# Summing rows of 1024 numbers: the input stream staged through two buffers of 24 rows in place of three of 16

## The chip, the cores and the metric

One NeuronCore of a Trainium2 chip runs the kernel. The metric is the device time of one execution in microseconds (us), taken as the median of several runs. The other cores are idle in these runs.

## The reference

```
x: float32 [32, 512, 1024], divisor = 1024
out[b, s] = sum(x[b, s, :]) / divisor        # float32 [32, 512]
```

So 16,384 rows of 1024 floats (4 KB each, 67.1 MB in all) are read, and one number per row is written.

## The kernel before, in words

The 16,384 rows are spread over the 128 partitions of the on-chip memory, 128 rows to a partition (`J = 128`). A partition's rows come from two places in the input: `F = 15` rows from a first region (`x_first`, where partition p starts p x 15 rows in), and `W = M + L = 113` rows from a second region (`x_main`, `M = 97` rows, followed for each partition by `x_last`, `L = 16` rows). In what follows "a row" means one row in each partition, that is 128 x 4 KB = 512 KB.

The input passes through three buffers, `bulk0` to `bulk2`, of 16 rows each (64 KB per partition). The list `loads` (lines 101 to 112) gives the order: 2 rows, five times 16 rows and 15 rows of the main region, then the 15 rows of the first region, then the last 16 rows cut in four: 10.6 rows (called `t8` in the code) and 3.7 rows (`t9`) into bulk buffers, and two small pieces, `pa` (5376 bytes per partition) and `pb` (1664 bytes), into buffers of their own. Each load names its buffer, one semaphore per buffer, its source, how many of its rows ScalarE sums (`on_act`: 4 of the last main load, 6 of the first region's load) and where the sums go.

There is no scheduler: each engine's queue is written out by hand, and semaphores order them.

- **SyncE (SP)** issues every DMA. The first two loads are moved ahead of the program's opening barrier (`start_loads_at_once`). Load 2 waits until load 0 has landed (line 138); from load 3 on, load k waits (lines 140 to 143) until the engines have finished with load k - 3, which held the same buffer. `pa` and `pb` follow load 9 with no wait of their own. Then SP waits for GpSimd and stores the first region's results, waits for `pa` and stores the main results, and waits for `done` and stores the last 16 columns.
- **VectorE (DVE)** takes the loads in order: one `reduce_sum` (line 215) per load over all its rows, less those that go to ScalarE. The last 16 rows are summed one at a time by `both_halves` (line 205), which adds the two halves of a row and accumulates.
- **ScalarE (ACT)** sums single rows by an activation with an accumulator (line 183): the `on_act` rows of two loads, and six of the last 16 rows.
- **GpSimd (POOL)** multiplies the finished sums by 1/1024 (lines 157 and 161).

Of the kernel before, what the change touches and what calls it, by code (L numbers as in the profile page):

```python
# [35 lines left out]
def kernel(  # L36
# [6 lines left out]
    nc = tc.nc  # L43
    nc.at_finalize(start_loads_at_once)
    xf = x.flatten_outer_dims()
    N, D = xf.shape
# [2 lines left out]
    J = N // P  # L49
    assert J * P == N  # L50

    F, L = 15, 16
    M = J - F - L
    W = M + L
    x_first = bass.AP(tensor=x.tensor, offset=0, ap=[[F * D, P], [1, F * D]])
# [1 line left out]
    x_last = bass.AP(tensor=x.tensor, offset=P * F * D + M * D, ap=[[W * D, P], [1, L * D]])  # L57
# [4 lines left out]
    def room(name, *shape):  # L62
        return nc.alloc_sbuf_tensor(name, [P, *shape], F32).ap()
# [2 lines left out]
    base = -(-nc.sbuf_base // 32) * 32  # L66
    room("pad", -base % 1024 // 4)
    assert nc.sbuf_base % 1024 == 0
    bulk = [room(f"bulk{i}", 16 * D) for i in range(3)]

# [2 lines left out]
    ends = [0, 10 * D + c10, 14 * D + c14, 15 * D + c15, 16 * D]  # L75
# [11 lines left out]
    loads = []  # L87
    sems = {}

    def sem(name):  # L90
        sems[name] = nc.alloc_semaphore(name)
        return sems[name]

    in_bulk = [sem(f"in_bulk{i}") for i in range(3)]
    in_pa, in_pb = (sem(f"in_{n}") for n in ("pa", "pb"))
    out_first, out_main = sem("out_first"), sem("out_main")
    dve, act, pool = sem("by_dve"), sem("by_act"), sem("by_pool")
    done = sem("done")
    landed = nc.alloc_semaphore("landed")

    main = [(2, 0)] + [(16, 0)] * 5 + [(15, 4)]
    first = [(15, 6)]
    assert sum(r for r, _ in first) == F and sum(r for r, _ in main) == M
    for rows_of, src, dst in ((main, x_main, res), (first, x_first, res0)):
        j = 0
        for rows, on_act in rows_of:
            t = bulk[len(loads) % 3][:, : rows * D]
            loads.append((t, in_bulk[len(loads) % 3], src[:, j * D : (j + rows) * D], on_act, dst[:, j : j + rows]))
            j += rows
    for k in range(2):  # L110
        t = bulk[len(loads) % 3][:, : ends[k + 1] - ends[k]]
        loads.append((t, in_bulk[len(loads) % 3], x_last[:, ends[k] : ends[k + 1]], 0, None))


    for t, s, src, *_ in loads[:2]:
        i = nc.sync.dma_start(out=t, in_=src).then_inc(s, 16)
        tc.no_tile_sem_insts.add(i.ins.name)
    tc.close()
    tc.compile()  # L119
# [2 lines left out]
    done_dve, done_act = {}, {}  # L122
# [4 lines left out]
    arrived, seen = [], {}  # L127
# [6 lines left out]
    for k, (t, s, src, *_) in enumerate(loads):  # L134
        if k < 2:
            continue
        if k == 2:
            nc.sync.wait_ge(loads[0][1], arrived[0])
        else:
            nc.sync.wait_ge(dve, done_dve[k - 3])  # L140
            if done_act[k - 3]:
                nc.sync.wait_ge(act, done_act[k - 3])
            nc.sync.wait_ge(s, arrived[k] - 16)
        nc.sync.dma_start(out=t, in_=src).then_inc(s, 16)
    nc.sync.dma_start(out=pa, in_=x_last[:, ends[2] : ends[3]]).then_inc(in_pa, 16)
    nc.sync.dma_start(out=pb[:, : D - c15], in_=x_last[:, ends[3] : ends[4]]).then_inc(in_pb, 16)
    nc.sync.wait_ge(pool, 3)
# [6 lines left out]
    k = len(main) - 1  # L154
# [31 lines left out]
    for k, (t, s, src, on_act, dst) in enumerate(loads[:-2]):  # L186
        rows = t.shape[1] // D
# [23 lines left out]
    for k, (t, s, src, on_act, dst) in enumerate(loads[:-2]):  # L211
        m = t.shape[1] // D - on_act
        nc.vector.wait_ge(s, arrived[k])
        rows = t[:, : m * D].rearrange("p (r d) -> p r d", d=D)
# [65 lines left out]
```

## Time and profile before

| what | value |
|---|---|
| median of three runs | 160.39 us (160.37 to 160.51) |
| span of the profiled execution, first to last instruction | 159.3 us |
| VectorE busy | 116.7 us (73%) |
| ScalarE busy | 18.6 us (12%) |
| DMA engines: packets, data, share of the span | 2160, 67.18 MB, 98.1% |
| mean rate over the span | 422 GB/s |

The profile is of one execution, and its page gives that execution's span but no time of its own for what lies outside the span. The median run is 1.1 us longer than the span (160.39 - 159.3); in what follows that 1.1 us is carried along unchanged.

The DMA engines' packets are also recorded one by one in the trace, with start, length and size. In these loads a packet is one descriptor: one partition's contiguous piece of a load, so a 16-row load is 128 packets of 65,536 bytes, eight for each of the 16 DMA engines. Eight is also the number of partitions that each engine serves.

### The profile page before, as it was taken

Reading aid. Unit: us, or ns where it says so; the run is one execution under the profiler, and the core shown is the slowest. Engines: PE = TensorE matmul, PEld = TensorE weight load, DVE = VectorE, ACT = ScalarE, POOL = GpSimd, SP = SyncE. Lnnn points to the kernel's source line nnn. Section 1 sums busy time; section 2 is a strip of 40 time slices with the busy share of each in tenths; the row PEclk is TensorE's granted clock in tenths of the full one; section 3 lists DMA queues with packets and bytes.
Section 4 is the critical chain, followed back from the end, with each engine's and each line's share of the span. In section 5 each row is a group of like instructions: output and inputs, shape, how many; then the busy total and the mean of one; then the engine's idle time right before and its main releaser. Section 6 shows DMA issues by size and latency. Waiting matters only on the chain.

```text
span 159.3 us, 144 instructions
## 1 busy us (share of the span) xinstructions
DVE 116.7 (73%) x32; ACT 18.6 (12%) x35; POOL 1.0 (1%) x7
## 2 busy tenths in 40 slices
DVE  0500009999499994999949999499989990399296
ACT  3000000000000000000000000000009100392196
POOL 0000000000000000000000000000000001000000
DMA  8996996996996997979969969969996999889894
GB/s 296 494 527 263 527 527 263 527 527 263 527 527 263 527 444 346 527 313 477 527 263 527 527 263 527 494 278 463 494 494 262 478 494 494 350 350 525 344 401 154
DMA packets 2160, 67.18 MB, mean 422 GB/s; under 512 B 624, under 2 KB 752, under 8 KB 880
## 3 DMA queue, kind: packets, MB, share of 16 engines
q1 hardware_dynamic: 2160, 67.18, 98.1%
HBM read 67.11 MB, written 0.07 MB: 422 GB/s over the span
## 4 chain that ended last, share of the span: by engine, by line
DMA 67%; DVE 30%; another core or an unknown queue 1%; issue 0%
DMA bulk<-in_x_dram 67%; DVE res L215 29%; DVE bulk L205 1%; DVE tail L205 0%; DVE pb L205 0%; DVE fin L205 0%
## 5 line engine op out<-in xcount | busy, mean ns | idle before, releaser
L215 DVE TENSOR_REDUCE res<-bulk 128x16 f32<-128x16384 f32 (+3 forms) x8 | 110.0, 13754 | 37.7 <-DMA bulk<-in_x_dram 37.7
L183 ACT ACTIVATE junk<-bulk 128x1024 f32<-128x1024 f32 (+1 forms) x16 | 15.6, 973 | 137.2 <-DMA bulk<-in_x_dram 137.2
L205 DVE CUSTOM_DVE_ANT_0 bulk<-bulk 128x512 f32<-128x512 f32 (+1 forms) x9 | 5.5, 665 | 3.1 <-DMA bulk<-in_x_dram 3.1
L183 ACT ACTIVATION_READ_ACCUMULATOR junk<-bulk 128x1 f32 x16 | 3.0, 187 | 0.0
L183 ACT ACT_TABLE_LOAD x1 | 1.3, 1283 | 1.9 <-PEq L119 1.9
L157 POOL TENSOR_SCALAR res<-res 128x97 f32<-128x97 f32 x1 | 0.5, 465 | 129.8 <-DVE res L215 129.8
L205 DVE DVE_READ_ACCUMULATOR2_ANT fin<- 128x1 f32 x10 | 0.8, 82 | 0.0
L183 ACT ACTIVATE junk<-tail 128x737 f32<-128x737 f32 x1 | 0.8, 789 | 0.0
L205 DVE CUSTOM_DVE_ANT_0 bulk<-bulk,part 128x192 f32<-128x192 f32 x1 | 0.4, 420 | 0.3 <-DMA bulk<-in_x_dram 0.3
L205 DVE CUSTOM_DVE_ANT_0 tail<-tail 128x304 f32<-128x304 f32 x1 | 0.5, 476 | 0.0
L205 DVE CUSTOM_DVE_ANT_0 pb<-pb 128x209 f32<-128x209 f32 x1 | 0.4, 379 | 0.1
L161 POOL TENSOR_SCALAR res<-res 128x15 f32<-128x15 f32 x1 | 0.3, 262 | 15.6 <-DVE res L215 15.6
L183 ACT ACTIVATION_READ_ACCUMULATOR junk<-tail 128x1 f32 x1 | 0.2, 187 | 0.0
L153 POOL MEMSET pb<- 128x2 f32 x1 | 0.1, 99 | 1.5 <-POOLq L119 1.5
L261 POOL MEMSET const-bfloat16-1.0<- 128x1 bf16 x1 | 0.1, 101 | 0.0
L261 POOL MEMSET const-uint8-127<- 128x1 uint8 x1 | 0.1, 101 | 0.0
L261 POOL MEMSET const-float32-0.0<- 128x1 f32 x1 | 0.1, 98 | 0.2 <-issue 0.2
L261 POOL MEMSET const-float32-1.0<- 128x1 f32 x1 | 0.1, 98 | 0.0
L205 DVE DVE_READ_ACCUMULATOR2_ANT pb<- 128x1 f32 x1 | 0.1, 84 | 0.0
L205 DVE DVE_READ_ACCUMULATOR2_ANT part<- 128x1 f32 x1 | 0.1, 83 | 0.0
## 6 DMA issues: line engine op xcount, KB each, us to landing
bulk<-in_x_dram SPq DMA_DIRECT2D x2, 7680.0 KB, 39.3
bulk<-in_x_dram SPq DMA_DIRECT2D x1, 5440.0 KB, 32.0
bulk<-in_x_dram SPq DMA_DIRECT2D x1, 1872.0 KB, 23.5
bulk<-in_x_dram SPq DMA_DIRECT2D x1, 1024.0 KB, 4.6
tail<-in_x_dram SPq DMA_DIRECT2D x1, 672.0 KB, 24.7
pb<-in_x_dram SPq DMA_DIRECT2D x1, 208.0 KB, 24.8
bulk<-in_x_dram SPq DMA_DIRECT2D x5, 40.8
out_dram<-res SPq DMA_DIRECT2D x1, 48.5 KB, 1.6
```

The source lines that it names most:

```text
L153: nc.gpsimd.memset(pb[:, D - c15 :], 0.0).then_inc(pool)
L157: nc.gpsimd.tensor_scalar_mul(out=res, in0=res, scalar1=scale).then_inc(pool)
L161: nc.gpsimd.tensor_scalar_mul(out=res0, in0=res0, scalar1=scale).then_inc(pool)
L183: nc.scalar.activation(scratch, src, COPY, scale=by, accum_out=dst).then_inc(count)
L205: return nc.vector.tensor_tensor_reduce(out=src[:, :h], in0=src[:, :h], in1=src[:, h:], scale=by, scalar=ahead, op0=ADD, op1=ADD, accum_ou ...
L215: nc.vector.reduce_sum(out=dst[:, :m], in_=rows, axis=AX).then_inc(dve)
L261: nc = _bacc.Bacc("TRN2", target_bir_lowering=False, num_devices=1)
```

## The change

The three buffers of 16 rows become two of 24 (192 KB per partition in all, as before). The loads become 2 rows, four times 24 rows of the main region, 14 rows of the first region, and the last 16 rows as they were: ten loads of input in place of twelve. A 24-row load is 96 KB per partition, and is written as an access pattern of two pieces of 48 KB. ScalarE sums 12 rows of the last 24-row load and 5 of the 14-row load. From load 2 on, load k waits for the engines to be done with load k - 2.

```diff
-    F, L = 15, 16
+    F, L = 14, 16
...
-    bulk = [room(f"bulk{i}", 16 * D) for i in range(3)]
+    bulk = [room(f"bulk{i}", 24 * D) for i in range(2)]
...
-    main = [(2, 0)] + [(16, 0)] * 5 + [(15, 4)]
-    first = [(15, 6)]
+    main = [(2, 0)] + [(24, 0)] * 3 + [(24, 12)]
+    first = [(14, 5)]
...
+    def load(t, src):
+        if t.shape[1] > 16 * D:
+            t, src = (v.rearrange("p (c f) -> p c f", c=2) for v in (t, src))
+        return nc.sync.dma_start(out=t, in_=src)
 
     for t, s, src, *_ in loads[:2]:
-        i = nc.sync.dma_start(out=t, in_=src).then_inc(s, 16)
+        i = load(t, src).then_inc(s, 16)
...
-        if k == 2:
-            nc.sync.wait_ge(loads[0][1], arrived[0])
-        else:
-            nc.sync.wait_ge(dve, done_dve[k - 3])
-            if done_act[k - 3]:
-                nc.sync.wait_ge(act, done_act[k - 3])
-            nc.sync.wait_ge(s, arrived[k] - 16)
-        nc.sync.dma_start(out=t, in_=src).then_inc(s, 16)
+        nc.sync.wait_ge(dve, done_dve[k - 2])
+        if done_act[k - 2]:
+            nc.sync.wait_ge(act, done_act[k - 2])
+        nc.sync.wait_ge(s, arrived[k] - 16)
+        load(t, src).then_inc(s, 16)
```

Elsewhere `% 3` becomes `% 2`. With F = 14, M becomes 98 and W becomes 114, so a partition's starting points in the input lie 114 rows (456 KB) apart in the second region in place of 113 (452 KB), and 14 rows (56 KB) in the first in place of 15 (60 KB). VectorE's instructions become one reduce of 2 rows, three of 24, one of 12 and one of 9, where they were 2, five of 16, 11 and 9; ScalarE sums 17 rows ahead of the last 16 where it summed 10. The work on the last 16 rows is the same, instruction for instruction.

More of the change, by code (lines that the diff above doesn't have):

```diff
@@ L92, in sem @@
         return sems[name]
-    in_bulk = [sem(f"in_bulk{i}") for i in range(3)]
+    in_bulk = [sem(f"in_bulk{i}") for i in range(2)]
     in_pa, in_pb = (sem(f"in_{n}") for n in ("pa", "pb"))
@@ L106 @@
         for rows, on_act in rows_of:
-            t = bulk[len(loads) % 3][:, : rows * D]
-            loads.append((t, in_bulk[len(loads) % 3], src[:, j * D : (j + rows) * D], on_act, dst[:, j : j + rows]))
+            t = bulk[len(loads) % 2][:, : rows * D]
+            loads.append((t, in_bulk[len(loads) % 2], src[:, j * D : (j + rows) * D], on_act, dst[:, j : j + rows]))
             j += rows
     for k in range(2):
-        t = bulk[len(loads) % 3][:, : ends[k + 1] - ends[k]]
-        loads.append((t, in_bulk[len(loads) % 3], x_last[:, ends[k] : ends[k + 1]], 0, None))
+        t = bulk[len(loads) % 2][:, : ends[k + 1] - ends[k]]
+        loads.append((t, in_bulk[len(loads) % 2], x_last[:, ends[k] : ends[k + 1]], 0, None))
+    def load(t, src):
+        if t.shape[1] > 16 * D:
+            t, src = (v.rearrange("p (c f) -> p c f", c=2) for v in (t, src))
+        return nc.sync.dma_start(out=t, in_=src)
     for t, s, src, *_ in loads[:2]:
-        i = nc.sync.dma_start(out=t, in_=src).then_inc(s, 16)
+        i = load(t, src).then_inc(s, 16)
         tc.no_tile_sem_insts.add(i.ins.name)
```

## The prediction

> **What bounds the kernel now.** I read the page's slices first, then its DMA table, then the packets in the trace. The slices show one resource that never rests:
>
> ```profile
> span 159.3 us, 144 instructions
> ...
> DVE  0500009999499994999949999499989990399296
> ...
> DMA  8996996996996997979969969969996999889894
> ...
> q1 hardware_dynamic: 2160, 67.18, 98.1%
> ```
>
> VectorE has holes (the 4s: it waits for each load). The DMA row's 6s are no holes: a 64 KB packet is booked in one slice and the slices are not multiples of it. Asked stage by stage (columns: stretch, its length, busy time of DVE, ACT and POOL, clock, DMA share, GB/s), the trace gives:
>
> ```profile
> 42.60:81.30 38.70, 34.44 (x2) 0.00 (x0) 0.00 (x0) 1.00 1.00 432
> ...
> 118.90:137.10 18.20, 11.89 (x1) 4.27 (x8) 0.47 (x1) 1.00 1.00 434
> ...
> 149.90:154.30 4.40, 3.48 (x11) 3.48 (x7) 0.00 (x0) 1.00 1.01 432
> ```
>
> The DMA share is 1.00 wherever loads follow loads, whether the load is 16 rows, 15 or 3.7. The timeline says what VectorE does meanwhile, and how the end hangs on the stream:
>
> ```profile
> 4.61 2.29 DVE L215 TENSOR_REDUCE res<-bulk 128x2 f32<-128x2048 f32 x1 [4.61 <-DMA bulk<-in_x_dram]
> ...
> 43.28 17.22 DVE L215 TENSOR_REDUCE res<-bulk 128x16 f32<-128x16384 f32 x1 [2.13 <-DMA bulk<-in_x_dram]
> 62.65 17.22 DVE L215 TENSOR_REDUCE res<-bulk 128x16 f32<-128x16384 f32 x1 [2.15 <-DMA bulk<-in_x_dram]
> ...
> 119.83 11.89 DVE L215 TENSOR_REDUCE res<-bulk 128x11 f32<-128x11264 f32 x1 [1.04 <-DMA bulk<-in_x_dram]
> ...
> 137.99 9.76 DVE L215 TENSOR_REDUCE res<-bulk 128x9 f32<-128x9216 f32 x1 [6.26 <-DMA bulk<-in_x_dram]
> ...
> 155.28 0.42 DVE L205 CUSTOM_DVE_ANT_0 bulk<-bulk,part 128x192 f32<-128x192 f32 x1 [0.29 <-DMA bulk<-in_x_dram]
> ...
> 157.85 0.33 SPq L238 DMA_DIRECT2D out_dram<-fin  x1
> ```
>
> Loads land 19.37 us apart (43.28 to 62.65) and are reduced in 17.22, so VectorE waits 2.1 us each time. From t9's landing at 155.28 a fixed string of work leads to the last store at 157.85 and the end of the span, 4.0 us after that landing. So the time is t9's landing + 4.0 + 1.1 outside the span, and the landing is set by the stream: when it starts, what each packet costs, and whether it pauses.
>
> **Packets.** In the trace's packet records the median lengths are 2.418 us for 65,536 bytes, 2.267 for 61,440, 1.608 for 43,520, 0.559 for 14,976, 0.309 for 8,192 and 0.069 for 1,664. A line through them: bytes / 27.2 GB/s + 0.008 us. Eight 64 KB packets are 19.344 us; the first packets of successive 16-row loads start at 23.24, 42.57, 61.96, 81.30, 100.67, that is 19.33 to 19.39 apart. Nothing is lost between loads: a load's border costs each engine some 0.007 us, its semaphore packet.
>
> **The change part by part.**
>
> *Removed and added packets.* Per partition the input was 12 packets (1 + 5 + 2 + 2 + 2) and becomes 14 (1 + 8 + 1 + 2 + 2). Two more, times eight partitions per engine, times 0.008 us: +0.13 us. Two load borders fewer: -0.01. The bytes are the same. The 48 KB packet is in no row; from its neighbours (43,520 and 61,440) the line gives 1.815 us, and 0.008 is what every size shows, so I take +0.12 us. Were its fixed part nil, the term would be -0.01; were it the 0.07 of a whole 1,664-byte packet, +1.0. I take the line because it holds over a forty-fold range of sizes.
>
> *Slow packets.* In the records some packets are longer than their median. Summed and shared over 16 engines that is 0.14 us in the 16-row loads (mean 2.4216 against 2.418, forty per engine), 0.18 in the two 15-row loads (2.278 against 2.267, sixteen), and about 0.03 in the rest of the stream. The new stream may have none (-0.35) or twice as many (+0.35). I see no reason for either and take 0.
>
> *The start.* Loads 0 and 1 still stand first. The trace's first packet starts at 1.00 us and load 1's at 3.92 us, while load 1 is issued by 0.85; a longer issue for its 256 packets has 3 us of cover. Load 2 now waits for load 0's reduce (6.9 us) instead of its landing (4.6); load 1 keeps the engines busy until 33, so 0.
>
> *The reduces.* 16 rows take 17.22 us and 2 rows 2.286: 1.067 a row and 0.15 fixed. So 24 rows take 25.75, 12 rows 12.95. VectorE saves some fixed parts, all in its own idle time: 0. ScalarE's 12 rows at 1.04 apart (12.5 us) stay under VectorE's 12.95, its 5 rows under 9.76: 0. GpSimd's two multiplies change by one column: 0.
>
> *The new waits.* This is the part that could cost. SP now issues load k + 1 only when load k - 1 is reduced, while load k is moving. Behind SP's wait stand all later loads; who suffers is the stream, if load k is out of packets before load k + 1's first one starts. Timed from load k - 1's last packet: 0.37 us until VectorE starts (the record of that packet's semaphore, 62.28, to 62.65), 25.75 for the reduce, 0.04 for SP to see it, and then issue to first packet. That last step the trace shows only on an idle queue: 1.00 us at the start, 0.83 at the last store (157.85 to 158.68). In sum 27.16. Load k has packets for 16 x 1.815 + 0.01 = 29.05 us, and the earliest engine is 0.32 ahead of the last (61.96 to 62.28): 28.73. **Slack 1.6 us.** Loads 3, 4 and 5 have this. Load 6 (t8) waits for 12 rows' reduce while the 14-row load moves (16.94 us): 2.3 us. Load 7 (t9) waits for 9 rows' reduce, 9.76, while t8 moves, 12.87: 12.87 - 0.32 - 0.37 - 9.76 - 0.04 - 1.00 = 1.4 us, the least. `pa` and `pb` are issued right behind t9, about 16 us later than before, and the first region's store after them; pb's issue ends about 1.3 us after t9's begins, and t9 only starts moving 2.4 us after its issue: 0. So I price the hand-offs at 0; if a busy queue takes over 2.4 us from issue to first packet, that is gone.
>
> *Strides.* A partition's pieces start 456 KB apart for 452, and 56 KB for 60. No row shows an even number of rows. The two strides shown, 113 and 15 rows, give 18.26 and 18.20 us of packets per engine for the two 15-row loads, 0.3% apart, and that is the bound either way: 0.3% of 154 us is 0.5 us. [...]
>
> [...]
>
> **Sum.** +0.12 + 0 + 0 + 0: 160.39 + 0.12 = 160.5 us; in the profile, t9 lands near 155.4 and the span is near 159.4. The median of a few runs tells about 0.2% (0.32 us) from nothing, so this is "the same".
>
> **Rivals.**
>
> 1. *The hand-off loses read-ahead* (slower). With one load queued instead of two, an engine crossing a load's border may have to ramp as it did at the start: there eight 8 KB packets took 2.935 us per engine and not 8 x 0.309 = 2.472, a loss of 0.46. At five late-issued loads that is 2.3 us: 162.8. For it: no row shows a load issued under 10 us ahead of its turn, besides the first two. Against it: 1.4 us are left, and the start's ramp also holds the first memory access of all. It decides from 2.4 us between issue and first packet. Chance 0.08.
> 2. *A loaded memory answers later* (slower). The 1.00 us from issue to first packet was on idle engines. Were it three times that while 16 engines stream, 3.0 us, three hand-offs would fall short by 0.4 (3.0 against 2.6) and t9's by 0.6: +1.8 us with the packets' 0.12 on top, 162.3. Twice, 2.0 us, would cost nothing. Against it: with 432 GB/s moving, borders cost nothing, though those loads were queued long before. Chance 0.06. [...]
> 3. *Strides or slow packets*, with their 0.3 to 0.5 us, shift the stream beyond what can be told: 161.0 with chance 0.08, 160.0 with chance 0.06.
> 4. *The descriptors are not two of 48 KB* but cut finer, say six of 16 KB: 4 loads x 8 partitions x 4 more x 0.008 = 1.0 us, 161.5. The built program shows the pattern 128x2x12288, which speaks for two. Chance 0.02.
>
> **How the numbers follow.** The forecast, no hand-off loss and packets on the line, has 0.70. Faster by over 0.2% is rival 3's lower end, 0.06; slower is 1, 2, 3's upper end and 4, with 0.24; within 0.2%, 0.70. The range takes the forecast's 160.1 to 160.8 and rival 3's ends, with small shortfalls of rivals 1 and 2 (a hand-off or two at 0.3 us): 160.0 to 161.2.
>
> **What would show it.** DMA packets 2384 in the table (2160 + 8 x 128 - 6 x 128 - 2 x 16); DMA share about 98%; 24-row reduces of about 25.75 us with VectorE idle 3.3 us before each; loads landing 29.05 us apart; 1.00 in every stretch between 4 and 154 us; t9's reduce at 155.4. I am wrong on the packets if loads are 29.05 apart plus more with the share still 1.00; on the hand-offs if the share falls under 1.00 around 33, 62, 91, 120, 137 or 150 us, where one load ends and the next begins.

## The result, and the profile after

The changed kernel takes 163.19 us (median of five runs, 162.87 to 163.55) against 160.39 us (160.36 to 160.75): slower by 1.7%, ratio 1.0172 with a 95% interval of 1.0157 to 1.0186. The forecast was 160.5 us with a range of 160.0 to 161.2.

The profiled run took 162.87 us, its span is 161.3 us. A second profile of the kernel before, taken with the last experiments, comes from a run of 160.40 us and has a span of 159.1 us. By the traces the spans are 161.34 and 159.07 us. So 2.3 of these 2.5 us lie in the span, and 0.2 outside of it (1.5 against 1.3 us), where the profile shows nothing. The comparison below uses this second profile where it needs a clean one: the first had some slow packets in its 15-row loads (2.278 us on average for a median of 2.267).

The page of the changed kernel:

```profile
span 161.3 us, 153 instructions
...
DVE  0500000069999974999999099999937994599185
...
DMA  8999999999999999999999999999999998989892
...
DMA packets 2384, 67.18 MB, mean 416 GB/s; under 512 B 592, under 2 KB 720, under 8 KB 848
...
q1 hardware_dynamic: 2384, 67.18, 97.5%
```

Read alone, this looks like what was forecast: 2384 packets, and a DMA row of nines to the end. A pause of a us on a few of 16 engines doesn't show in slices of 4 us. VectorE's instructions do show it, since each of its reduces starts when the last of the 16 engines has brought its part (load 3's last packet ends at 92.45 in the packet records, and its reduce starts at 92.80; the number in brackets is VectorE's idle time before):

```profile
33.72 25.75 DVE L217 TENSOR_REDUCE res<-bulk 128x24 f32<-128x24576 f32 x1 [26.71 <-DMA bulk<-in_x_dram]
62.70 25.75 DVE L217 TENSOR_REDUCE res<-bulk 128x24 f32<-128x24576 f32 x1 [3.24 <-DMA bulk<-in_x_dram]
92.80 25.75 DVE L217 TENSOR_REDUCE res<-bulk 128x24 f32<-128x24576 f32 x1 [4.35 <-DMA bulk<-in_x_dram]
121.83 12.95 DVE L217 TENSOR_REDUCE res<-bulk 128x12 f32<-128x12288 f32 x1 [3.27 <-DMA bulk<-in_x_dram]
139.13 9.75 DVE L217 TENSOR_REDUCE res<-bulk 128x9 f32<-128x9216 f32 x1 [4.35 <-DMA bulk<-in_x_dram]
152.47 0.49 DVE L207 CUSTOM_DVE_ANT_0 bulk<-bulk 128x320 f32<-128x320 f32 x1 [3.58 <-DMA bulk<-in_x_dram]
157.10 0.42 DVE L207 CUSTOM_DVE_ANT_0 bulk<-bulk,part 128x192 f32<-128x192 f32 x1 [0.46 <-DMA bulk<-in_x_dram]
```

Load 2, the last one issued early, lands 28.98 us after load 1, as 16 packets of 1.815 us per engine should. Load 3, the first one issued late, takes 30.10 (+1.1); load 4 29.03; the 14 rows 17.30 (+0.4 on 8 x 2.117); t8 13.34 and t9 4.63, where the second profile of before has 12.83 and 4.42 (+0.5 and +0.2). Together that is about the 2.1 us by which t9 lands later, at 157.10 against 155.01; from there to the end of the span it is 4.2 us against 4.1. What these five have in common is that they were issued late. The chain that ended last passes through three of them, loads 3, 5 and t9 (start, length, what):

```profile
33.72 25.76 DVE res L217
59.48 0.02 issue
59.49 33.28 DMA bulk<-in_x_dram
92.78 0.02 issue
92.80 25.77 DVE res L217
118.57 0.02 issue
118.59 20.52 DMA bulk<-in_x_dram
139.11 0.02 issue
139.13 9.77 DVE res L217
148.90 0.02 issue
148.91 8.16 DMA bulk<-in_x_dram
```

The chain goes from a reduce to the issue of the next load but one, and from the issue to that load's landing. Before, such a stretch began at an issue some 20 us ahead of the load's turn; in the first profile's chain, that of load 6 (15 rows) is

```profile
79.89 39.92 DMA bulk<-in_x_dram
```

of which its own packets are 18.3 us. In the changed kernel's three stretches, take off each load's own packets (29.05, 16.94, 4.47) and the 0.37 us until VectorE starts, and what is left of 33.28, 20.52 and 8.16 is 3.9, 3.2 and 3.3 us: the time from SP's issue until the slowest engine moves the load at its full rate. The prediction had 1.00 us there, from issue to first packet.

The packet records show the same place from the other side. In load 4, issued at 88.49 with the stream reaching it at 91.18, 15 of the first 48 packets are late: 14 of them are long, up to 2.23 us for a median of 1.815, and one starts 0.5 us after its engine's last one ended. (The records don't name the engine; packets were strung together by their ends and starts. "Late" is used below for packets over 0.04 us longer than their size's median, or starting over 0.03 us after the one before, among the first 48 of a load. "Lead" is the time from a load's issue to the first packet of it that any engine starts.) The leads of loads 3 to 7 were 2.5, 2.7, 1.7, 2.4 and 1.2 us. The engines are not alike in this: in load 5, by the same stringing, 13 of the 16 engines lost nothing, with only 1.7 to 2.9 us between the issue and their own turn, and the other three lost 0.2 to 0.8 us. The landing goes by the last engine to end, at 138.81 where the first ends at 137.22; VectorE's reduce starts at 139.13.

### The profile page after: what moved, and what is told of

Same layout as the page of the kernel before. It is cut to its first block, busy times and chain, and to the rows that moved or that the text cites. A ratio compares the mean times of both kernels' runs of the same rounds, so it can differ in the third digit from the quotient of the medians.

```text
span 161.3 us, 153 instructions
## 1 busy us (share of the span) xinstructions
DVE 108.9 (68%) x30; ACT 25.9 (16%) x49; POOL 1.0 (1%) x7
## 2 busy tenths in 40 slices
DMA packets 2384, 67.18 MB, mean 416 GB/s; under 512 B 592, under 2 KB 720, under 8 KB 848
## 3 DMA queue, kind: packets, MB, share of 16 engines
q1 hardware_dynamic: 2384, 67.18, 97.5%
## 4 chain that ended last, share of the span: by engine, by line
DMA 59%; DVE 38%; ACT 1%; issue 1%; SPq 0%
DMA bulk<-in_x_dram 59%; DVE res L217 38%; ACT junk L185 1%; SPq L118 0%
## 5 line engine op out<-in xcount | busy, mean ns | idle before, releaser
L217 DVE TENSOR_REDUCE res<-bulk 128x24 f32<-128x24576 f32 (+3 forms) x6 | 102.3, 17042 | 46.6 <-DMA bulk<-in_x_dram 46.6
L185 ACT ACTIVATE junk<-bulk 128x1024 f32<-128x1024 f32 (+1 forms) x23 | 22.6, 983 | 131.7 <-DMA bulk<-in_x_dram 131.7
L185 ACT ACTIVATION_READ_ACCUMULATOR junk<-bulk 128x1 f32 x23 | 4.3, 187 | 0.0
L159 POOL TENSOR_SCALAR res<-res 128x98 f32<-128x98 f32 x1 | 0.5, 465 | 132.8 <-DVE res L217 132.8
```

Of the source, the lines that this page charges most:

```text
L159: nc.gpsimd.tensor_scalar_mul(out=res, in0=res, scalar1=scale).then_inc(pool)
L185: nc.scalar.activation(scratch, src, COPY, scale=by, accum_out=dst).then_inc(count)
L217: nc.vector.reduce_sum(out=dst[:, :m], in_=rows, axis=AX).then_inc(dve)
```

## The experiments

Theory A is what this reading suggests: a load issued only some 3 us ahead of its turn reaches some engines late. Rivals: B, the strides of 114 and 14 rows make packets slow; C, only t9 and the small transfers behind it suffer. All ratios are to the kernel before, with 95% intervals.

**1. ScalarE helps, so that loads 3 to 5 are issued earlier.**

```diff
-    main = [(2, 0)] + [(24, 0)] * 3 + [(24, 12)]
+    main = [(2, 0)] + [(24, 8)] * 3 + [(24, 12)]
```

> ScalarE takes 8 rows of each of the first three 24-row loads, so VectorE's reduce there is 16 rows (about 17.2 us instead of 25.75) and SP issues loads 3, 4 and 5 about 11.8 us before the load ahead of them has landed, instead of 3.2. t9 is still issued late. Theory A (a load issued only some 3 us ahead of its turn reaches some of the 16 DMA engines late, and these stay behind to the end): the slow first packets at 62, 91 and 120 us go, the loads' landings stay 29.05 apart, and the time falls by 1.0 to 1.5 us from 163.2, to 161.7 to 162.2, the rest staying with t9. Theory B (the row strides of 114 and 14 make packets slow): unchanged, 163.2. Theory C (only the late issue of t9 and of the small transfers behind it costs): unchanged, 163.2.

Measured: 162.27 us, 1.0109 (1.0092 to 1.0127). That is just above the 161.7 to 162.2 that A gave. Leads of loads 3 to 5 are 10.9 us and none of their first 48 packets is late. What stays is at the end: t8 lands 13.77 us after the 14 rows (+0.9) and t9 4.71 after t8 (+0.3). B and C both said 163.2; C can still be right in part.

**2. t9 behind t8 in the same buffer, so that t9, pa and pb are issued early.**

```diff
+        s = in_bulk[len(loads) % 2]
+        if k == 1:
+            t, s = bulk[0][:, ends[1] : ends[2]], in_t9
...
+        if k < len(loads) - 1:
             nc.sync.wait_ge(dve, done_dve[k - 2])
```

> t9 goes into the free part of bulk0 behind t8, with a semaphore of its own, so t9, pa and pb are issued right behind t8 near 135 us instead of 149 us; loads 3, 4 and 5 are issued as late as in the changed kernel. Theory A: t9's slow packets (up to 0.92 us against 0.559) go, the time falls by 0.5 to 0.9 us, to 162.3 to 162.7. Theory B: unchanged, 163.2. Theory C: all of the loss goes, 160.5.

Measured: 162.79 us (161.52 to 163.18), 1.0129 (1.0101 to 1.0158), 0.1 us above the 162.3 to 162.7 that A gave, with the runs far apart. t8 and t9 now land 12.84 and 4.46 us apart, without loss, but in this profile the 14-row load, with a lead of 1.6 us, lost 1.6 (121.97 to 140.50 is 18.53). VectorE's rows and the DMA share around it (columns as in the prediction):

```profile
121.97 12.95 DVE L222 TENSOR_REDUCE res<-bulk 128x12 f32<-128x12288 f32 x1 [3.39 <-DMA bulk<-in_x_dram]
...
140.50 9.76 DVE L222 TENSOR_REDUCE res<-bulk 128x9 f32<-128x9216 f32 x1 [5.57 <-DMA bulk<-in_x_dram]
```

```profile
93.50:119.50 26.00, 25.08 (x1) 0.00 (x0) 0.00 (x0) 1.00 0.98 423
119.50:122.50 3.00, 0.53 (x1) 0.53 (x1) 0.00 (x0) 1.00 1.05 377
122.50:125.00 2.50, 2.50 (x1) 2.50 (x5) 0.00 (x0) 1.00 0.75 275
```

The share of 0.75 between 122.5 and 125 proves little by itself, since a whole packet is booked in one window and these windows are short. The kernel before reads 0.76 where its packet records show no wait over 0.2 us:

```profile
119.50:122.50 3.00, 2.67 (x1) 2.67 (x5) 0.00 (x0) 1.00 0.76 328
```

What shows the loss is the landing, 18.53 us after load 4's, and the packet records, by which all 16 engines lost on this load, 0.5 to 2.0 us each. C falls: with t9 mended most of the loss remains.

**3. Both edits.**

> Both edits: no load is issued less than about 5 us ahead of its turn. Theory A: 160.4 to 160.7, the packets' own 0.1 us being all that is left. Theory B: unchanged, 163.2. Theory C: 160.5, the same as with t9 alone moved.

Measured: 160.82 us, 1.0028 (1.0016 to 1.0040). B falls, since the strides are those of the change: about five sixths of the 2.8 us are gone with them in place. 0.1 us more than A's upper end is left. Part of what is left can't come from a short lead: load 4, issued 10.9 us ahead, landed 29.39 us after load 3 (29.28 in experiment 1), because a few packets in its later part were slow. Why they were, no run here shows.

**4. The strides of before, the late issues of the change.**

```diff
-    F, L = 14, 16
+    F, L = 15, 16
...
-    main = [(2, 0)] + [(24, 0)] * 3 + [(24, 12)]
-    first = [(14, 5)]
+    main = [(2, 0)] + [(24, 0)] * 3 + [(23, 12)]
+    first = [(15, 6)]
```

> The strides of the kernel before (113 rows in the second region, 15 in the first), with two buffers of 24 rows and late issues as in the changed kernel; the last main load is 23 rows and the first region's 15. Theory A: unchanged, 163.0 to 163.4. Theory B: 160.4 to 160.7. Theory C: unchanged.

Measured: 165.85 us, 1.0314 (1.0279 to 1.0350), which neither theory said. The old strides help nothing, against B. That it got slower has a reason that the edit brought along: load 4 has 23 rows and moves 1.2 us less, while load 5 still waits for 24 rows' reduce. Its lead fell to 1.0 us, with 32 late packets and gaps of up to 2.9 us on single engines, and it landed 20.43 us after load 4 (+2.3 on 18.14).

**5 and 6. How much lead is enough: one row or two rows on ScalarE.** As experiment 3, with `(24, 1)` and `(24, 2)` for `(24, 8)`.

> As the kernel with both edits (t9 behind t8, ScalarE helping with the first three 24-row loads), but ScalarE takes 1 row of each of these loads instead of 8. SP issues loads 3, 4 and 5 about 3.5 us before the stream reaches them (2.4 with no row, 10.9 with eight). Theory A, sharpened from the packet records (on the slowest engine a load issued into a busy queue needs 3.3 to 3.9 us until its first packet moves at full rate, not 1.0): most of the loss goes, a few late packets are left; 160.9 to 161.6. If the queue must instead hold several packets ahead (a need that grows with the lead, not a threshold): 161.8 to 162.2.

> The same with 2 rows on ScalarE: lead about 4.6 us, above the 3.9 us. Theory A with the threshold: as with eight rows, 160.7 to 160.9, and no late first packets at 62, 91 and 120 us. A need that grows with the lead: 161.3 to 161.7.

Measured: 160.67 us, 1.0016 (1.0007 to 1.0026) with one row, and 160.82 us, 1.0028 (1.0016 to 1.0041) with two. One row is as good as eight, and better than the 160.9 to 161.6 that A gave. With it the three leads are 3.41 to 3.47 us and no packet of the three loads is late:

```profile
62.79 24.69 DVE L222 TENSOR_REDUCE res<-bulk 128x23 f32<-128x23552 f32 x1 [4.32 <-DMA bulk<-in_x_dram]
91.84 24.69 DVE L222 TENSOR_REDUCE res<-bulk 128x23 f32<-128x23552 f32 x1 [4.36 <-DMA bulk<-in_x_dram]
120.83 12.95 DVE L222 TENSOR_REDUCE res<-bulk 128x12 f32<-128x12288 f32 x1 [4.30 <-DMA bulk<-in_x_dram]
```

The loads land 29.05 and 28.99 apart. 1.07 us of reduce per load (25.75 to 24.69) with t9 moved is worth 2.5 us. So the need for many packets in the queue, which would have left 161.8 to 162.2, falls: about 3.4 us of lead was enough, where 2.3 to 2.7 us lost 0.3 to 1.1 us on load 3 (the change and experiments 2, 4, 8 and 9). The border isn't sharp. t8's lead of 3.1 us in these two runs cost 0.3 and 0.4 us, while t8 in experiment 3 (lead 2.7) and the 14 rows in experiment 9 (lead 2.4) landed without loss.

**7. The reverse: the kernel before, issuing one load later.**

```diff
-            nc.sync.wait_ge(dve, done_dve[k - 3])
-            if done_act[k - 3]:
-                nc.sync.wait_ge(act, done_act[k - 3])
+            nc.sync.wait_ge(dve, done_dve[k - 2])
+            if done_act[k - 2]:
+                nc.sync.wait_ge(act, done_act[k - 2])
```

> The kernel before (three buffers of 16 rows, strides 113 and 15) with one change: load k waits for the engines to be done with load k - 2, as in the changed kernel, though a third buffer lies free. A 16-row load moves for 19.35 us and is reduced in 17.22, so the lead is about 1.4 us. Theory A: a load that starts 2 us late gives the next one 2 us more lead, so about every other of six hand-offs loses some 2 us on its slowest engines: 163.5 to 166.5, with gaps of 1 to 3 us in the packet records where loads meet. Theory B (strides, packet sizes or two buffers as such): unchanged, 160.4.

Measured: 166.87 us, 1.0389 (1.0348 to 1.0430), a little above the expected range. Three buffers, 64 KB packets and the old strides are all in place; the wait alone costs 6.5 us, over twice what the whole change does, with leads of 1.0 to 1.9 us (6.0 for t8):

```profile
43.28 17.22 DVE L215 TENSOR_REDUCE res<-bulk 128x16 f32<-128x16384 f32 x1 [2.11 <-DMA bulk<-in_x_dram]
63.02 17.22 DVE L215 TENSOR_REDUCE res<-bulk 128x16 f32<-128x16384 f32 x1 [2.52 <-DMA bulk<-in_x_dram]
82.53 17.22 DVE L215 TENSOR_REDUCE res<-bulk 128x16 f32<-128x16384 f32 x1 [2.30 <-DMA bulk<-in_x_dram]
103.89 17.22 DVE L215 TENSOR_REDUCE res<-bulk 128x16 f32<-128x16384 f32 x1 [4.14 <-DMA bulk<-in_x_dram]
```

Load 5 was issued at 80.26, when load 3's reduce ended, and landed at 103.89: 23.63 us, less 19.35 for its packets and 0.37, is 3.9 us again. The even alternation of lost and kept hand-offs that was expected is not in the trace.

**8 and 9. Smaller packets.** Is the delay the 48 KB packet that an engine has to finish first (theory H)? Experiment 8 writes the 24-row load as six pieces (`c=6`):

> The changed kernel with each 24-row load cut into six pieces of 16 KB instead of two of 48 KB; waits and leads unchanged. Its packets cost 4 loads x 8 x 4 more x 0.008 = 1.0 us. Theory H (the delay from issue to first packet is the time of the 48 KB packet that each engine has to finish, 1.8 us, before it sees new work): hand-offs lose nothing, 161.4 to 161.7, and no first packet is late. Theory A without H (the delay does not depend on the packets' size): the loss of the changed kernel stays and the packets' 1.0 comes on top, 163.8 to 164.4.

The packet records show 1024 packets of 49,152 bytes, and the DMA instructions in the trace already have two pieces of that size per partition: the six adjoining pieces had become two, so this run says nothing on H. It is a second sample of the changed kernel: 163.04 us, 1.0164 (1.0117 to 1.0211). Experiment 9 keeps the pieces apart with 32 bytes of room after every four rows:

```diff
-    bulk = [room(f"bulk{i}", 24 * D) for i in range(2)]
+    Q = 4 * D + 8
+    bulk = [room(f"bulk{i}", 6 * Q) for i in range(2)]
...
+            if rows == 24:
+                t = bulk[len(loads) % 2].rearrange("p (c q) -> p c q", q=Q)[:, :, : 4 * D]
```

> The changed kernel with 32 bytes of room left in the buffers after every four rows, so that a 24-row load cannot be moved in longer pieces than 16 KB: six packets per partition and load. Waits are those of the changed kernel; a 24-row load moves about 0.25 us longer (32 more packets per engine at 0.008 us), so the lead is that much more. Theory H (an engine sees new work only when its packet is done, so the delay of some 3.5 us follows the packets' size): hand-offs into 24-row loads lose nothing, 161.6 to 162.6, what is left being the packets' 1.0 and the hand-offs at the end. Theory A without H: late first packets at 62, 91 and 120 us as before, 163.3 to 164.5.

Measured: 163.74 us, 1.0222 (1.0179 to 1.0266), inside what A without H gave and above H's range. Yet of the packets after 62, 91 and 121 us only 1, 1 and 0 were late (2, 15 and 3 in the change), with leads of 2.7, 2.7 and 2.4. The profile's loss sits at the end, behind the 56 KB and 42.5 KB packets that were not cut: t9 landed 5.58 us after t8 (+1.2). One profile, with slightly longer leads, doesn't settle H.

**10. Does load 1's longer list slow the start?** In several profiles of 24-row kernels load 0 is seen at 4.8 to 5.0 us, against 4.61 before. As experiment 5, with load 1 of 16 rows:

```diff
-    main = [(2, 0)] + [(24, 1)] * 3 + [(24, 12)]
+    main = [(2, 0)] + [(16, 2)] * 3 + [(24, 1), (24, 12)]
```

> As the kernel with one ScalarE row per 24-row load and t9 behind t8 (160.67), but the first three of the four 24-row loads' rows and the fourth's are split as three loads of 16 rows (two rows of each on ScalarE, to keep the lead near 3.5 us) and two of 24, so that load 1 has 128 packets instead of 256 when load 0 starts. Theory S (the 256 descriptors of load 1, issued 0.43 us after load 0, slow load 0's first packets): load 0 is seen at 4.60 to 4.65 instead of 4.68 to 5.01, and the time falls by about 0.2 us, to 160.4 to 160.5. Else: 160.6 to 160.7.

Measured: 160.84 us, 1.0035 (1.0023 to 1.0048), load 0 at 4.90; the time is above what either side expected. Theory S falls, and the second profile of before has load 0 at 4.80 by itself: the start varies from run to run. Here t8 landed 13.27 us after the 14 rows, +0.4.

**11. t8 earlier too.** t8 goes to the rear of `bulk0` and t9 to its front; ScalarE takes 11 rows of the last 24-row load, and t8 waits for these alone.

```diff
-    main = [(2, 0)] + [(24, 1)] * 3 + [(24, 12)]
+    main = [(2, 0)] + [(24, 1)] * 3 + [(24, 11)]
...
+        t = bulk[0][:, 24 * D - ends[1] :]
...
+            t, s = bulk[0][:, : ends[2] - ends[1]], in_t9
```

> As the kernel with one ScalarE row per 24-row load and t9 behind t8, but t8 goes to the rear of bulk0 and t9 to its front, and ScalarE takes 11 rows of the last 24-row load, so that t8 waits for ScalarE's 11 rows only (about 11.5 us) and its lead is about 4.5 us instead of 3.1. Theory A: no late first packets at 137 us (there are 2 to 10 of them with leads of 2.4 to 3.1), time 160.5 to 160.65. Else 160.7.

Measured: 160.43 us, 1.0006 (0.9994 to 1.0018), no different from the kernel before, and just under the 160.5 to 160.65 that A gave. t8's lead is 4.6 us, and none of its packets is late; in experiments 5, 6 and 10 it was 3.0 to 3.1, and t8 took 0.3 to 0.4 us over its time in all three. With two buffers of 24 rows kept and every lead at 3.4 us or more, the change costs nothing that can be told. Its landings against the second profile of before:

```profile
137.73 9.75 DVE L225 TENSOR_REDUCE res<-bulk 128x9 f32<-128x9216 f32 x1 [2.89 <-DMA bulk<-in_x_dram]
150.57 0.49 DVE L215 CUSTOM_DVE_ANT_0 bulk<-bulk 128x320 f32<-128x320 f32 x1 [3.09 <-DMA bulk<-in_x_dram]
155.07 0.42 DVE L215 CUSTOM_DVE_ANT_0 bulk<-bulk,part 128x192 f32<-128x192 f32 x1 [0.33 <-DMA bulk<-in_x_dram]
```

```profile
137.76 9.76 DVE L215 TENSOR_REDUCE res<-bulk 128x9 f32<-128x9216 f32 x1 [6.32 <-DMA bulk<-in_x_dram]
150.59 0.49 DVE L205 CUSTOM_DVE_ANT_0 bulk<-bulk 128x320 f32<-128x320 f32 x1 [3.08 <-DMA bulk<-in_x_dram]
155.01 0.42 DVE L205 CUSTOM_DVE_ANT_0 bulk<-bulk,part 128x192 f32<-128x192 f32 x1 [0.25 <-DMA bulk<-in_x_dram]
```

**12. The kernel before once more.**

> The kernel before once more, for a second profile of it with its own time: load 0 seen near 4.6 us and the time outside the span near 1.1 us if the first profile is typical; near 4.8 and 1.4 if these differ from run to run.

160.40 us; its span and landings are used above. The time outside its span is 1.3 us, so the 1.1 of the prediction was 0.2 short.

## Why the prediction was wrong

*The step that failed* is in "The new waits": "that last step the trace shows only on an idle queue: 1.00 us at the start". It was carried to a busy queue, and gave a slack of 1.6 us. The rest of the sum held: it leaves 2.6 us between load 3's or 4's issue and its turn, and the leads were 2.5 and 2.7. But the delay that this lead had to cover was taken too short. On the slowest engine it is 3.2 to 3.9 us in the changed kernel (4.6 in experiment 2's 14-row load, by 140.50 - 118.61 - 16.94 - 0.37). With 3.9 the same sum is 28.73 - 0.37 - 25.75 - 0.04 - 3.9 = -1.3 us for loads 3 and 4, or -1.0 for an engine that comes to the border last, without the 0.32; load 3 lost 1.1, on such an engine. Two errors are in the 1.00. It was read from the first packet of the fastest engine, while the landing goes by the slowest: load 0's own landing, 4.58 - 0.37 - 2.47 of packets, gives 1.7 even at the start. And behind a queue that was moving data, the slowest engine took another 1.5 to 2.2 us (3.2 to 3.9 less 1.7).

*The bound was named and not used.* The text put the limit at 2.4 us and gave rivals 1 and 2 a chance of 0.14 together, at 162.8 and 162.3; the result lies above both, by 0.4 and 0.9 us. Both were hand-offs that lose; rival 2's 3.0 us was the nearer in size to the 3.2 to 3.9. A term that no row shows, bounded between 1.00 and 3.0 with the sum changing sign at 2.4, does not carry a chance of 0.70 for one side. That a loaded memory makes the delay, as rival 2 has it, no run here shows.

*A second thing the sum left out:* a late engine stayed late, and its lateness ate the next lead. The two engines that lost time at load 3's start, by the same stringing 0.6 and 0.8 us, ended it last, at 92.10 and 92.45 us, and ended load 4 last, at 121.15 and 121.47. Load 3's last packet came 1.1 us late, so VectorE began its reduce at 92.80 and load 5 was issued with 1.7 us of lead, where loads 3 and 4 had 2.5 and 2.7; the other 14 engines had lost nothing at load 3's start. In the end t9 was issued with 1.2. The hand-offs were priced one by one.

*The sign that was named didn't serve.* The share was to fall under 1.00 where loads meet. In windows of 2.5 to 3 us there it reads 0.85 to 1.20 in the changed kernel, and windows at the same times read 0.76 to 1.11 in the kernel before. The distance of the landings showed the loss.

*What held:* the packet count, 2384, is exact. 24-row loads with enough lead, from load 2 on, land 28.96 to 29.07 us apart, for 29.05, but for load 4 of experiments 1 and 3. The 16 KB pieces lengthened a load from 29.00 to 29.30 us, 0.30 for 32 more packets per engine, for the 0.25 expected; but that is near by luck. In the packet records each packet starts 0.003 to 0.004 us before the last one ends, so its fixed part costs about 0.005 us and not 0.008, which makes 0.15; the rest is packets longer than their median. In the prediction's +0.12 us this error is 0.05. For the strides the sum has 0, which no run had shown for strides of 114 and 14 rows; the runs show no cost of them: experiment 11's stream reaches t8 at 136.95 us, the second profile of before at 136.91. The reduces (25.75, 12.95) came out to the hundredth and cost nothing by themselves. The forecast of no difference is what experiment 11 measures, with the leads that the change does not give.

## What to carry to other kernels

In a stream that keeps the DMA engines full, count for each load the time from its issue to its turn, and compare it with the time from issue to full rate that a loaded queue shows on its slowest engine (3.2 to 3.9 us in the changed kernel), not with the first packet of an idle one (1.00 us); here 3.4 us was enough, and 2.7 us or less in most cases was not. Two buffers of 24 rows in place of three of 16, the same size in all, shortened that lead here from some 20 us to 1.2 to 2.7, though the reduce (25.75 us) is faster than the load (29.05), because with two buffers the lead is only the difference between the two. When the trace has no row for a short lead, make one: delaying one wait in the kernel at hand (experiment 7) would have shown it.

## What the runs showed of the hardware

- The 16 DMA engines did not share out a delay in the changed kernel. By the stringing each moved 16 packets of every 24-row load, and load 4's two latest engines began it at 92.10 and 92.45 us and ended it at 121.15 and 121.47, where the first one ended at 120.30. VectorE's reduce of the whole load started at 121.83, while the DMA share reads 1.00 from 93.5 to 119.5 us and 0.86 from 119.5 to 122.5.
- A 24-row load written as six adjoining 16 KB pieces reached the DMA engines as two packets of 48 KB per partition (1024 packets of 49,152 bytes in experiment 8); with 32 bytes of room between the pieces it came as 16 KB packets (4432 packets in all in experiment 9, 2048 more than the 2384 of the change).
- What is left open: what the 3.2 to 3.9 us consist of, why they differ from engine to engine, whether they follow the packet's size, and the 0.2 to 0.3 us more outside the span in the changed kernel.
